# A hybrid decoder block with an expert mixer: which chunks take the dense path, and where the last two chunks are selected

## The chip, the core and the metric

The kernel runs on one core of a Trainium2 chip. Its engines work side by side, each through its own queue in order: TensorE (PE, with PEld for its weight loads), VectorE (DVE), ScalarE (ACT), GpSimd (POOL) and the queue that issues most DMAs (SP). The metric is the device time of one execution in microseconds.

## What is computed

The input is 1024 tokens of width 1024, with 16 meta tokens in front. A mixer (a causal convolution beside a latent attention, both normalised, times `w_out`) is added to the input; the rest is the expert mixer, which works on chunks of 128 tokens:

```python
q = (xb @ wq).reshape(C, PEER_HEADS, 2, PEER_DK_HALF)
s = jnp.einsum('chpd,hpnd->chpn', q, keys).astype(jnp.float32)
sv, si = lax.top_k(s, K)
cand = sv[:, :, 0, :, None] + sv[:, :, 1, None, :]
cidx = si[:, :, 0, :, None] * N_KEYS + si[:, :, 1, None, :]
top_s, sel = lax.top_k(cand.reshape(C, PEER_HEADS, K * K), K)
eidx = jnp.take_along_axis(cidx.reshape(C, PEER_HEADS, K * K), sel, axis=-1)
g = jax.nn.softmax(top_s, axis=-1)
u = u_tab[eidx]
act = jax.nn.gelu(jnp.einsum('chkd,cd->chk', u, xb).astype(jnp.float32), approximate=False)
w = (g * act).astype(xb.dtype)
return jnp.einsum('chk,chkd->cd', w, v_tab[eidx])
```

So each token picks 128 of 16384 experts (8 heads, 16 each), takes a dot product with each expert's row of u, and sums the rows of v with the weights. A last norm with the gain `g_final` follows.

## The kernel before, in words

The eight chunks are worked on in five sets (chunk 0; chunk 1; chunks 2 and 3; 4 and 5; 6 and 7). The string `ORDER` (line 61) says in which order the program is recorded: B is the attention of a set, C its output projection with the scores and the first top 16 (`mix_out`), S its selection (`select`: candidate sums, the second top 16, and the look-up of the expert numbers by comparison `eq` on VectorE, product `ep` on GpSimd and reduction `ef` on VectorE), T its turn (`turn`: the numbers transposed). A scheduler then places each instruction in its engine's queue, by this order and by its own estimate of times; within a queue the order is fixed.

The experts are evaluated in two ways. The chunks in `GATHER` fetch rows: `gather_u` has GpSimd issue, for each of 128 places, an indirect DMA of one row of u per token (`ug`, three buffers), and VectorE multiplies and sums it (`ujunk`, line 691); `gather_v` fetches the rows of v (`vg`, seven buffers) and TensorE sums them (`gv`, line 718). A chunk's v runs beside the next chunk's u; `finish` scales and stores the chunk.

The chunks in `DENSE` take all 16384 experts: E (`expand`) makes a dense table of their gates (VectorE and GpSimd build one-hot factors `one`, `two`, `ah`, `al`, TensorE multiplies them into `pg`, ScalarE copies to `st`, and a DMA writes `g_d`). Then `dense` runs over 128 blocks of 128 experts: `pa` = u times the tokens (24 matmuls of three products of split operands), gelu, times the gates (`ge`, line 818), split into `wh` and `wl` (lines 821 and 822), and after each four blocks `pv` = v times the weights (96 matmuls), added to `acc` on VectorE (line 835). The operands are split (`u_..l`, `v_..l`, line 784) on VectorE. All dense chunks of a block go through one matmul of 512 columns. The gathers run on beside it, 1.1 steps a block as recorded (`RATE`), 32 steps before it (G32).

Before, chunks 0 to 3 are gathered and chunks 4 to 7 dense, so the dense part needs the selection and expansion of the last set.

Of the kernel before, what the change touches and what calls it, by code (L numbers as in the profile page):

```python
# [13 lines left out]
F32 = mybir.dt.float32  # L14
F32R = mybir.dt.float32r
# [20 lines left out]
H = 8  # L36
# [23 lines left out]

ORDER = "B1 C1 S1 B2 C2 T1 S2 B3 C3 T2 S3 B4 X0 C4 T3 E0 E1 Y0 S4 T4 E2 N0 E3 U3 G32 D0"
RATE = 1.1
CONV_POOL = [3]
GATHER = [0, 1, 2, 3]
DENSE = [4, 5, 6, 7]
ND = len(DENSE) * P
# [16 lines left out]
def trunk_kernel(ctx, tc, x, meta, g_mix, w_ab, w_lat, g_q, w_uq, g_kv, w_ukv, conv_w, conv_b,  # L83
# [469 lines left out]
    def mix_out(si, MT):  # L553
# [22 lines left out]

        sv = [sel.tile([P, H, 2, TK], F32, name=f"sv{si}_{j}", tag="sv", bufs=dim.nw) for j in range(nt)]
        sx = [sel.tile([P, H, 2, TK], U32, name=f"sx{si}_{j}", tag="sx", bufs=dim.nw) for j in range(nt)]
        for h in range(H):
# [29 lines left out]

    def select(c, sv, sx):  # L610
        si = sel.tile([P, H, 2, TK], F32, name=f"si{c}", tag="sif", bufs=1)
        V.tensor_copy(si, sx)
# [17 lines left out]
        e = sel.tile([P, H, TK], F32, name=f"ef{c}", tag="ef", bufs=dim.nw)  # L630
        for h in range(0, H, HB):
            for i, n in enumerate((NC1, NCAND)):
                ks = slice(8 * i, 8 * i + 8)
                sh = [P, HB, n, 8]
                eq = sel.tile(sh, F16, name=f"eq{c}_{h}_{i}", tag=f"eq{i}", bufs=2)
                pr = sel.tile(sh, F32, name=f"ep{c}_{h}_{i}", tag=f"ep{i}", bufs=2)
                V.tensor_tensor(eq, tf[:, h:h + HB, None, ks].broadcast_to(sh), iota_c[:, None, :n].broadcast_to(sh), op=OP.is_equal)  # L637
                G.tensor_tensor(pr, eq, cidx[:, h:h + HB, :n, None].broadcast_to(sh), op=OP.mult)
                V.tensor_reduce(e[:, h:h + HB, ks], pr.rearrange("p h c k -> p h k c"), axis=AX.X, op=OP.add)  # L639
        g = sel.tile([P, H, TK], F32, name=f"gg{c}", tag="gg", bufs=dim.nw)  # L640
        gs = sel.tile([P, H], F32, name=f"gs{c}", tag="gs", bufs=1)
# [15 lines left out]
    def turn(c):  # L657

        ef, g = picks[c]
        tp = bank(f"et{c}", (P, 4, P), "s" if c in DENSE else "c")  # L660
        transpose_to(tp[:, 0], ef, P)
        eT = const.tile([P, P], I32, name=f"eT{c}", tag="eT", bufs=5)
        V.tensor_copy(eT, tp[:, 0])
        if c in GATHER:
            chunks[c] += (eT,)
        else:
            transpose_to(tp[:, 1], g.rearrange("p h k -> p (h k)"), P)
            t = sel.tile([P, 4, P], F16, name=f"gd{c}", tag="gd", bufs=len(DENSE))
# [27 lines left out]
    def gather_v(c):  # L696
# [36 lines left out]

    def finish(c, ht):
# [52 lines left out]
    def dense_u(i1, bank):  # L787
# [9 lines left out]
        return ge  # L797

    def dense():
        dn = ctx.enter_context(tc.tile_pool(name="dn", bufs=1, **RW))  # L800
        psd = ctx.enter_context(tc.tile_pool(name="psd", bufs=1, space=PSUM, **RW))

        def pbank(name):
# [6 lines left out]
        for g in range(NK // NG):  # L810
# [3 lines left out]
            for b in range(NG):  # L814
                i1 = NG * g + b
                ge = ges.pop(0) if ges else dense_u(i1, pbank)
                gev = ge.rearrange("p (a t) -> p a t", t=TG)
                V.tensor_tensor(gev, gev, gt[:, :, b], op=OP.mult)
                wh = dn.tile([P, ND], F32R, name=f"wh{i1}", tag="wh", bufs=5)
                wl = dn.tile([P, ND], F32R, name=f"wl{i1}", tag="wl", bufs=4)  # L820
                A.activation(wh, ge, AF.Copy)  # L821
                V.tensor_tensor(wl, ge, wh.bitcast(F32), op=OP.subtract)  # L822
                W.append((wh, wl))
                while done < RATE * (i1 + 1):
                    next(steps, None)
                    done += 1
# [45 lines left out]
    for t in tops[0]:  # L872
        select(*t)
# [5 lines left out]
    dim = SimpleNamespace(nw=NW, nk=NC, wraw=WRAW)  # L879
# [3 lines left out]
    gp = ctx.enter_context(tc.tile_pool(name="gp", bufs=1, side="right", **RW))  # L883
    sel = select_pool()
# [7 lines left out]
    for step in ORDER.split():  # L892
# [90 lines left out]
```

## Time and profile before

| | us |
|---|---|
| median of 3 runs (3037.05 to 3041.81) | 3037.69 |
| the profiled execution | 3034.4 |
| its span in the profile | 3032.6 |
| busy: PE, DVE, ACT, POOL | 2591.0, 2165.6, 1009.9, 1589.2 |
| chain that ended last: PE, DVE, DMA | 49%, 17%, 12% |

The shares of busy time are means over stages with different limits; the slices of the page's second part show TensorE at 5 to 7 tenths in the second quarter and at 9 from the middle on. Matmuls are pipelined, and one has 0.39 us of latency where the next starts earlier, so their pace is read from the distance of starts. A row of `gv` or `ujunk` in the program leaves two records in the trace.

### The profile page before, as it was taken

To read this page: it belongs to the slowest core of one execution; us is meant where nothing else is said; L and a number is where in the kernel's file an instruction comes from. 1 tells how busy PE (TensorE), PEld (TensorE's weight loads), DVE (VectorE), ACT (ScalarE), POOL (GpSimd) and SP (SyncE) were. 2 spreads that over 40 slices of the span, in tenths; PEclk is the share of its full clock that TensorE was granted. 3 is DMA by queue.
4 is the path that set the end of the run, shared out by engine and by line. 5 is a ranking of instruction groups with operands and counts; after the bars stand their busy time and mean duration, and the time that the engine had idled before them with its cause. 6 is when DMAs were issued, how large, how long until landed. Compare 5 with 4: busy or idle time off the path is not lost.

```text
span 3032.6 us, 40483 instructions
## 1 busy us (share of the span) xinstructions
PE 2591.0 (85%) x13295; PEld 1932.6 (64%) x13295; DVE 2165.6 (71%) x4917; ACT 1009.9 (33%) x2200; POOL 1589.2 (52%) x1608
## 2 busy tenths in 40 slices
PE   6878669897876756558998999999999999999996
PEld 6775547776643534336877777777777777776663
DVE  4888857999998999876877766666676656653332
ACT  5435325352520433443222222322232322232221
POOL 5885453534568668662333544544555444534444
PEclk9888858898897877668999999999999999999998
DMA  4114789896788996998888999999999999978886
GB/s 141 46 49 144 227 257 322 261 295 225 246 280 288 314 305 228 315 307 316 300 297 285 326 356 348 332 347 335 346 334 345 337 343 339 352 282 318 311 308 215
DMA packets 372563, 858.36 MB, mean 283 GB/s; under 512 B 37952, under 2 KB 134400, under 8 KB 368256
## 3 DMA queue, kind: packets, MB, share of 16 engines
q0 software_dynamic: 147456, 536.94, 50.9%
q1 hardware_dynamic: 216528, 295.68, 28.7%
q10 hardware_dynamic: 8368, 23.15, 2.1%
q8 instruction: 105, 1.72, 0.2%
q14 instruction: 106, 0.87, 0.1%
HBM read 798.92 MB, written 56.71 MB: 282 GB/s over the span
## 4 chain that ended last, share of the span: by engine, by line
PE 49%; DVE 17%; DMA 12%; issue 4%; POOL 3%; ACT 1%; POOLq 0%; DVEq 0%; ACTq 0%; SPq 0%
PE pv L178 19%; PE pa L178 18%; DMA ug<-in_dram,ei 9%; PE gv L718 7%; DVE ujunk L691 4%; DVE ef L639 2%; DMA vg<-in_dram,eT 1%; PE op L564 1%; DVE two L753 1%; DVE eq L637 1%; DVE ah L755 1%; POOL vg L714 1%; DVE one L754 1%; POOL ug L688 1%; POOL al L756 1%
## 5 line engine op out<-in xcount | busy, mean ns | idle before, releaser
L714 POOL DMA_INDIRECT vg<-in_dram,eT x512 | 559.5, 1093 | 652.6 <-PE gv L718 520.0
L688 POOL DMA_INDIRECT ug<-in_dram,ei x512 | 553.7, 1081 | 584.4 <-DVE ujunk L691 299.6
L691 DVE SCALAR_TENSOR_TENSOR ujunk<-ug,xn 128x1024 bf16<-128x1024 f32 x512 | 638.4, 1247 | 149.4 <-DMA ug<-in_dram,ei 139.1
L835 DVE TENSOR_TENSOR acc<-acc,pv 128x512 f32<-128x512 f32 x256 | 171.9, 685 | 203.5 <-PE pv L178 176.1
L718 PE MATMUL gv<-vg,wd 128*32 128x512 f32 x2048 | 275.6, 653 | 37.5 <-DMA vg<-in_dram,eT 37.4
L178 PE MATMUL pv<-v_0h,wh 128*128 128x512 f32 x512 | 201.3, 398 | 23.9 <-ACT wh L821 16.9
L178 PE MATMUL pv<-v_1l,wh 128*128 128x512 f32 x512 | 200.9, 394 | 3.7 <-DVE v_1l L784 3.7
L178 PE MATMUL pa<-xdh,u_1l 128*128 128x512 f32 x512 | 200.8, 392 | 2.5 <-DVE u_1l L784 2.5
L178 PE MATMUL pa<-xdh,u_0h 128*128 128x512 f32 x512 | 202.1, 395 | 0.3 <-ACT st L764 0.3
L178 PE MATMUL pa<-xdl,u_0h 128*128 128x512 f32 x512 | 201.3, 393 | 0.0
L178 PE MATMUL pa<-xdh,u_0l 128*128 128x512 f32 x512 | 201.2, 393 | 0.0
L178 PE MATMUL pa<-xdh,u_1h 128*128 128x512 f32 x512 | 201.0, 393 | 0.2 <-ACT u_1h L783 0.2
L178 PE MATMUL pa<-xdl,u_1h 128*128 128x512 f32 x512 | 200.4, 391 | 0.0
L178 PE MATMUL pv<-v_0l,wh 128*128 128x512 f32 x512 | 200.3, 395 | 0.0
L178 PE MATMUL pv<-v_1h,wl 128*128 128x512 f32 x512 | 199.9, 392 | 0.0
L178 PE MATMUL pv<-v_1h,wh 128*128 128x512 f32 x512 | 196.5, 396 | 2.8 <-DVE acc L835 2.8
L783 ACT ACTIVATE u_1h<-u_1r 128x512 fp32r<-128x512 f32 x128 | 80.7, 631 | 349.6 <-PE pa L178 251.1
L178 PE MATMUL pv<-v_0h,wl 128*128 128x512 f32 x512 | 194.7, 395 | 0.8 <-DVE wl L822 0.8
L764 ACT ACTIVATE st<-pg 128x256 f32<-128x256 f32 x256 | 130.1, 644 | 190.0 <-PE pg L762 140.7
L783 ACT ACTIVATE u_0h<-u_0r 128x512 fp32r<-128x512 f32 x128 | 80.8, 631 | 322.4 <-PE pa L178 244.9
L761 PE MATMUL pg<-ah,two 128*128 128x128 f16 x512 | 98.0, 271 | 98.2 <-DVE ah L755 82.8
L784 DVE TENSOR_TENSOR u_0l<-u_0r,u_0h 128x512 fp32r<-128x512 f32 x128 | 88.5, 692 | 126.6 <-ACT u_0h L783 89.7
(449 smaller groups left out, 5910.1 us busy)
## 6 DMA issues: line engine op xcount, KB each, us to landing
g_d<-st SPq DMA_DIRECT2D x32, 1024.0 KB
u_0r<-in_dram SPq DMA_DIRECT2D x128, 256.0 KB
u_1r<-in_dram SPq DMA_DIRECT2D x128, 256.0 KB
gt<-g_d SPq DMA_DIRECT2D x32, 1024.0 KB
v_0r<-in_dram SPq DMA_DIRECT2D x128, 256.0 KB
v_1r<-in_dram SPq DMA_DIRECT2D x128, 256.0 KB
wo<-in_dram SPq DMA_DIRECT2D x80, 256.0 KB
wq<-in_dram SPq DMA_DIRECT2D x80, 256.0 KB
```

Source lines behind the costliest of these rows:

```text
L178: PE.matmul(dst, l, r, start=first and j == 0, stop=last and j == 2)
L564: PE.matmul(pb, MT[:, k, j * P:(j + 1) * P], w[k // 2][:, k % 2], start=k == 0, stop=k == KD - 1)
L639: V.tensor_reduce(e[:, h:h + HB, ks], pr.rearrange("p h c k -> p h k c"), axis=AX.X, op=OP.add)
L688: G.indirect_dma_start(out=ug, out_offset=None, in_=u_tab, in_offset=bass.IndirectOffsetOnAxis(ap=ei[:, j:j + 1], axis=0))
L691: V.scalar_tensor_tensor(junk, ug, 1.0, xn, op0=OP.mult, op1=OP.mult, accum_out=dots[:, j:j + 1])
L714: G.indirect_dma_start(out=vg[j], out_offset=None, in_=v_tab, in_offset=bass.IndirectOffsetOnAxis(ap=eT[:, t:t + 1], axis=0))
L718: PE.matmul(acc[32 * j:32 * j + 32, 512 * n:512 * n + 512], w[:, j, 32 * i:32 * i + 32], vg[j][:, 512 * n:512 * n + 512], start=q == 0 and ...
L761: PE.matmul(pg[:, k], two[:, a, :, b], ah[:, a, :, b], start=True, stop=False)
L764: A.activation(st[i][:, :, r0 + r:r0 + r + 4].rearrange("p a b -> p b a"), pg[:, :, i * NK // 2:(i + 1) * NK // 2], AF.Copy, scale=1.0 / G ...
L783: A.activation(hi, raw, AF.Copy)
L784: V.tensor_tensor(lo, raw, hi.bitcast(F32), op=OP.subtract)
L835: V.tensor_tensor(a, a, pv, op=OP.add)
```

## The change

Chunks 2 to 5 become dense, and 0, 1, 6 and 7 are gathered. The expansions E0 to E3 are recorded before the projection of the last set (C4), and S4 and T4 leave the string: the last set's selection, `late_set`, is a generator that the dense part advances twice after each block's `wl`, and `tc.issue_after` ties these steps in order behind that `wl`. Its first-round values live in a pool of their own (`late`), and `select` yields between its pieces. In the dense part the selection's buffers for comparison and product are single, the turn's transposes use the banks of `pa`, and `wh` has four buffers instead of five. The final gain is no longer kept on chip: it is loaded for each gathered chunk, and once for the dense ones, into a buffer of `vg`. The diff, cut:

```diff
-ORDER = "B1 C1 S1 B2 C2 T1 S2 B3 C3 T2 S3 B4 X0 C4 T3 E0 E1 Y0 S4 T4 E2 N0 E3 U3 G32 D0"
+ORDER = "B1 C1 S1 T1 B2 C2 S2 B3 C3 S3 B4 X0 T2 T3 E0 E1 E2 E3 C4 Y0 N0 U3 G32 D0"
...
-GATHER = [0, 1, 2, 3]
-DENSE = [4, 5, 6, 7]
+GATHER = [0, 1, 6, 7]
+DENSE = [2, 3, 4, 5]
+LATE = 4
...
         for h in range(H):
+            if h % 2 == 0:
+                yield
             top16(tv[:, h], ti[:, h], cand[:, h], NCAND)
+        yield
...
         for h in range(0, H, HB):
+            if h and h % 2 == 0:
+                yield
             for i, n in enumerate((NC1, NCAND)):
...
-                eq = sel.tile(sh, F16, name=f"eq{c}_{h}_{i}", tag=f"eq{i}", bufs=2)
-                pr = sel.tile(sh, F32, name=f"ep{c}_{h}_{i}", tag=f"ep{i}", bufs=2)
+                eq = sel.tile(sh, F16, name=f"eq{c}_{h}_{i}", tag=f"eq{i}", bufs=dim.sb)
+                pr = sel.tile(sh, F32, name=f"ep{c}_{h}_{i}", tag=f"ep{i}", bufs=dim.sb)
...
-        tp = bank(f"et{c}", (P, 4, P), "s" if c in DENSE else "c")
+        tp = bank(f"et{c}", (P, 4, P), "c")
...
-        finish(c, ht)
+        finish(c, ht, load_bcast(gp.tile([P, D], F32, name=f"gfin{c}", tag="vg", bufs=7), g_fin))
...
+    def late_set():
+        for t in tops[LATE]:
+            for _ in select(*t):
+                yield
+            turn(t[0])
+
     def dense():
...
+        banks["c"] = (psd, 3, "act")
+        rest = late_set()
...
-                wh = dn.tile([P, ND], F32R, name=f"wh{i1}", tag="wh", bufs=5)
+                wh = dn.tile([P, ND], F32R, name=f"wh{i1}", tag="wh", bufs=4)
...
-                V.tensor_tensor(wl, ge, wh.bitcast(F32), op=OP.subtract)
+                split_done = V.tensor_tensor(wl, ge, wh.bitcast(F32), op=OP.subtract)
                 W.append((wh, wl))
+                with tc.issue_after(split_done.ins):
+                    next(rest, None)
+                    next(rest, None)
                 while done < RATE * (i1 + 1):
...
+        gfin = load_bcast(gp.tile([P, D], F32, name="gfin", tag="vg", bufs=7), g_fin)
         for ci, c in enumerate(DENSE):
-            finish(c, acc[:, ci])
+            finish(c, acc[:, ci], gfin)
...
-    gfin = load_bcast(gp.tile([P, D], F32, name="gfin"), g_fin)
...
             ps_ctx.close()
+            dim.sb = dim.sp = 1
+            sel = ctx.enter_context(tc.tile_pool(name="sel", bufs=1, side="right", **RW))
             dense()
```

Where the instructions stand, at three places. First VectorE's queue at the first dense blocks; `wl0` is the low split of block 0's weights, `v0_1_0l` a split of v, `ge3` block 3's product with the gates, `ujunk` a gathered row, `pv0_0_0` a sum of block group 0. Before:

```order
L784 TENSOR_TENSOR v0_0_0l_12209<-v0_0_0r_12207,v0_0_0h_12208 128x512
L822 TENSOR_TENSOR wl0_11979<-ge0_11366,wh0_11978 128x512
L822 TENSOR_TENSOR wl1_12059<-ge1_11405,wh1_12058 128x512
L784 TENSOR_TENSOR v0_1_0l_12215<-v0_1_0r_12213,v0_1_0h_12214 128x512
L822 TENSOR_TENSOR wl2_12096<-ge2_11444,wh2_12095 128x512
L691 SCALAR_TENSOR_TENSOR ujunk_14342,dots1_12008<-ug1_91_14340,xn1_12006 128x1024
L784 TENSOR_TENSOR v0_2_0l_12221<-v0_2_0r_12219,v0_2_0h_12220 128x512
L818 TENSOR_TENSOR ge3_12168<-ge3_12168,gt0_11975 128x512
L784 TENSOR_TENSOR v0_3_0l_12227<-v0_3_0r_12225,v0_3_0h_12226 128x512
```

After (`si6`, `cand6` are the selection of chunk 6):

```order
L839 TENSOR_TENSOR wl0_11651<-ge0_11035,wh0_11650 128x512
L616 CAST si6_11654<-sx4_0_10571 128x256
L624 TENSOR_TENSOR cand6_11656<-sv4_0_10569 128x8x8
L624 TENSOR_TENSOR cand6_11656<-sv4_0_10569 128x8x4 x3
L624 TENSOR_TENSOR cand6_11656<-sv4_0_10569 128x8x8
L624 TENSOR_TENSOR cand6_11656<-sv4_0_10569 128x8x4
L624 TENSOR_TENSOR cand6_11656<-sv4_0_10569 128x8x3
L624 TENSOR_TENSOR cand6_11656<-sv4_0_10569 128x8x2 x2
L624 TENSOR_TENSOR cand6_11656<-sv4_0_10569 128x8x3
L624 TENSOR_TENSOR cand6_11656<-sv4_0_10569 128x8x8
L839 TENSOR_TENSOR wl1_11770<-ge1_11074,wh1_11769 128x512
L793 TENSOR_TENSOR v0_1_0l_12019<-v0_1_0r_12017,v0_1_0h_12018 128x512
```

Between the splits of blocks 0 and 1 there now stand a cast and the eleven candidate sums of chunk 6's selection; its further pieces, and chunk 7's, follow between the later splits up to block 9.

Second TensorE's queue at block 5; `pa5` is block 5's first product, `pv1` the sum of blocks 4 to 7, `et6` the transpose of chunk 6's expert numbers. Before:

```order
L178 MATMUL pa4_12369<-xdh_9918,u4_1l_12390 128x512
L178 MATMUL pa4_12369<-xdh_9918,u4_1h_12389 128x512
L178 MATMUL pa4_12369<-xdl_9919,u4_1h_12389 128x512
L178 MATMUL pa4_12369<-xdh_9918,u4_1l_12390 128x512
L178 MATMUL pa5_12445<-xdh_9918,u5_0h_12447 128x512
L178 MATMUL pa5_12445<-xdl_9919,u5_0h_12447 128x512
L178 MATMUL pa5_12445<-xdh_9918,u5_0l_12448 128x512
```

After:

```order
L180 MATMUL pv1_0_1_12682<-v1_0_0h_12645,wl4_12214 128x512
L180 MATMUL pv1_0_2_12696<-v1_0_0h_12645,wh4_12213 128x512
L180 MATMUL pv1_0_2_12696<-v1_0_0l_12646,wh4_12213 128x512
L180 MATMUL pv1_0_2_12696<-v1_0_0h_12645,wl4_12214 128x512
L158 MATMUL et6_12247<-ident_111,ef6_11842 128x128
L180 MATMUL pa5_12322<-xdh_10921,u5_0h_12324 128x512
L180 MATMUL pa5_12322<-xdl_10922,u5_0h_12324 128x512
```

The transpose of the selection's result stands ahead of block 5, and chunk 7's in the same way ahead of block 9; before, both stood ahead of block 3, at the start of the last two expansions.

Third the end of VectorE's queue; `os` are the roots for the final scaling, `ht` the last gathered chunk. Before:

```order
L835 TENSOR_TENSOR acc_11970<-acc_11970,pv31_1_2_26337 128x512
L835 TENSOR_TENSOR acc_11970<-acc_11970,pv31_1_3_26351 128x512
L724 TENSOR_TENSOR ht3_25387<-ht3_25387,gv3_22294 128x1024
L736 SCALAR_TENSOR_TENSOR ht3_25387<-ht3_25387,os3_25391,gfin_3872 128x1024
L736 SCALAR_TENSOR_TENSOR acc_11970<-acc_11970,os4_26366,gfin_3872 128x1024
L736 SCALAR_TENSOR_TENSOR acc_11970<-acc_11970,os5_26373,gfin_3872 128x1024
L736 SCALAR_TENSOR_TENSOR acc_11970<-acc_11970,os6_26380,gfin_3872 128x1024
```

After:

```order
L855 TENSOR_TENSOR acc_11642<-acc_11642,pv31_1_1_26335 128x512
L855 TENSOR_TENSOR acc_11642<-acc_11642,pv31_1_2_26349 128x512
L745 SCALAR_TENSOR_TENSOR acc_11642<-acc_11642,os2_26380,gfin_26377 128x1024
L745 SCALAR_TENSOR_TENSOR acc_11642<-acc_11642,os3_26387,gfin_26377 128x1024
L855 TENSOR_TENSOR acc_11642<-acc_11642,pv31_1_3_26363 128x512
L745 SCALAR_TENSOR_TENSOR acc_11642<-acc_11642,os4_26394,gfin_26377 128x1024
L745 SCALAR_TENSOR_TENSOR acc_11642<-acc_11642,os5_26401,gfin_26377 128x1024
```

The last gathered chunk's sum and scaling stood behind the last dense sum and ahead of the dense chunks' scalings; now they stand earlier in the queue, before block 127, and two scalings stand ahead of the last dense sum.

## Rows read from the trace of the kernel before

**Rows 1.** windows by stage: length, busy PE, PEld, DVE, ACT, POOL, clock, DMA

```profile
600.00:882.00 282.00, 243.39 (x1260) 188.81 (x1262) 260.04 (x1021) 125.73 (x371) 135.18 (x156) 0.90 0.83 266
882.00:947.00 65.00, 33.25 (x144) 15.96 (x136) 60.76 (x270) 4.30 (x11) 53.77 (x63) 0.74 0.75 251
947.00:1070.00 123.00, 86.64 (x554) 63.20 (x554) 107.51 (x287) 40.06 (x85) 89.91 (x83) 0.84 0.91 314
1070.00:1210.00 140.00, 81.92 (x535) 54.64 (x536) 136.82 (x436) 48.74 (x98) 101.24 (x104) 0.71 0.78 259
1210.00:1292.00 82.00, 42.97 (x321) 25.45 (x320) 65.77 (x94) 31.56 (x63) 53.81 (x44) 0.66 0.95 318
1292.00:1360.00 68.00, 38.79 (x318) 25.12 (x317) 53.36 (x76) 30.26 (x61) 42.97 (x33) 0.63 0.93 302
1360.00:1397.00 37.00, 21.77 (x104) 16.44 (x104) 15.67 (x24) 7.61 (x15) 15.87 (x14) 0.82 1.00 368
1397.00:1456.00 59.00, 55.88 (x239) 46.14 (x240) 47.39 (x79) 21.68 (x38) 15.72 (x14) 0.94 0.82 287
1456.00:1651.00 195.00, 179.83 (x762) 143.92 (x761) 155.15 (x261) 52.10 (x94) 73.63 (x68) 0.98 0.86 292
1651.00:2994.40 1343.40, 1336.14 (x6509) 970.28 (x6507) 798.47 (x1291) 373.12 (x628) 636.85 (x591) 1.00 0.92 330
2994.40:3032.60 38.20, 9.15 (x49) 1.60 (x48) 8.33 (x7) 5.75 (x10) 13.14 (x17) 0.64 0.54 196
```

**Rows 2.** the windows of line 818 alone: length, busy DVE (x begun), clock, DMA

```profile
1397.00:1456.00 59.00, 5.79 (x9) 0.94 0.82 287
1456.00:1651.00 195.00, 10.25 (x15) 0.98 0.86 292
```

**Rows 3.** who waited for whom, VectorE, 1397 to 1651 us: total, times, longest

```profile
DVE ujunk L691 <- DMA ug<-in_dram,ei: 39.8, 27, 5.7
```

**Rows 4.** VectorE in order of time, the end: start, duration, operation, idle before

```profile
2994.66 0.69 DVE L835 TENSOR_TENSOR acc<-acc,pv 128x512 f32<-128x512 f32 x1 [2.07 <-PE pv L178]
3015.49 1.22 DVE L724 TENSOR_TENSOR ht<-ht,gv 128x1024 f32<-128x1024 f32 x1 [20.15 <-PE gv L718]
3018.90 1.28 DVE L736 SCALAR_TENSOR_TENSOR ht<-ht,os,gfin 128x1024 f32<-128x1024 f32 x1 [2.18 <-POOL os L141]
...
3026.07 1.28 DVE L736 SCALAR_TENSOR_TENSOR acc<-acc,os,gfin 128x1024 f32<-128x1024 f32 x1 [0.44 <-POOL os L141]
```

**Rows 5.** the window of chunk 0's selection: columns as in rows 1

```profile
364.30:390.50 26.20, 1.76 (x9) 1.76 (x9) 24.87 (x107) 0.31 (x1) 14.28 (x28) 0.50 0.63 194
```

**Rows 6.** window of the rows of u (tile ujunk) alone, as rows 2

```profile
1456.00:1651.00 195.00, 82.33 (x134) 0.98 0.86 292
```

**Rows 7.** groups by line, VectorE: busy us, mean ns, idle before by releaser

```profile
L822 DVE TENSOR_TENSOR wl<-ge,wh 128x512 fp32r<-128x512 f32 x128 | 87.9, 689 | 48.5 <-ACT wh L821 33.1 <-PE pv L178 8.7 <-issue 6.4
L818 DVE TENSOR_TENSOR ge<-ge,gt 128x512 f32<-128x512 f32 x128 | 87.3, 685 | 21.5 <-ACT ge L796 12.0 <-DMA gt<-g_d 9.2 <-issue 0.3
```

**Rows 8.** who waited for whom, VectorE, 1210 to 1360 us

```profile
DVE one L754 <- POOL al L756: 26.0, 5, 7.0
```

**Rows 9.** who waited for whom, VectorE, 880 to 1210 us

```profile
DVE ef L639 <- POOL ep L638: 6.4, 4, 5.1
```

**Rows 10.** window of the gather matmuls (tile gv) alone: PE, PEld, DVE first

```profile
1651.00:2994.40 1343.40, 181.87 (x1504) 39.34 (x1504) 3.65 (x3) 1.00 0.92 330
```

**Rows 11.** groups by line, GpSimd: columns as in rows 7

```profile
L688 POOL DMA_INDIRECT ug<-in_dram,ei x512 | 553.7, 1081 | 584.4 <-DVE ujunk L691 299.6 <-issue 59.8 <-DVE mx L505 29.6
L638 POOL TENSOR_TENSOR ep<-eq,cidx 128x160 f32<-128x160 f16 (+1 forms) x128 | 103.7, 823 | 33.5 <-DVE eq L637 32.3 <-DVE tv L604 0.3 <-DVE gs L645 0.2
```

**Rows 12.** TensorE in order of time, first dense matmuls: start, duration

```profile
1369.23 0.63 PE L178 MATMUL pa<-xdh,u_0l 128*128 128x512 f32 x1
1369.66 0.46 PE L178 MATMUL pa<-xdh,u_0h 128*128 128x512 f32 x1
1369.96 0.40 PE L178 MATMUL pa<-xdl,u_0h 128*128 128x512 f32 x1
```

More of the change, by code (lines that the diff above doesn't have):

```diff
@@ L575, in mix_out @@
             to_T(hs[j], P, NT, j * P)
-        sv = [sel.tile([P, H, 2, TK], F32, name=f"sv{si}_{j}", tag="sv", bufs=dim.nw) for j in range(nt)]
-        sx = [sel.tile([P, H, 2, TK], U32, name=f"sx{si}_{j}", tag="sx", bufs=dim.nw) for j in range(nt)]
+        pool = late if si == LATE else sel
+        sv = [pool.tile([P, H, 2, TK], F32, name=f"sv{si}_{j}", tag="sv", bufs=dim.nw) for j in range(nt)]
+        sx = [pool.tile([P, H, 2, TK], U32, name=f"sx{si}_{j}", tag="sx", bufs=dim.nw) for j in range(nt)]
         for h in range(H):
@@ L626, in select @@
         for h in range(H):
+            if h % 2 == 0:
+                yield
             top16(tv[:, h], ti[:, h], cand[:, h], NCAND)
+        yield
         tf = sel.tile([P, H, TK], F16, name=f"tf{c}", tag="tf", bufs=1)
         V.tensor_copy(tf, ti)
[L630 removed]
+        e = sel.tile([P, H, TK], F32, name=f"ef{c}", tag="ef", bufs=dim.sp)
         for h in range(0, H, HB):
+            if h and h % 2 == 0:
+                yield
             for i, n in enumerate((NC1, NCAND)):
@@ L639, in select @@
                 V.tensor_reduce(e[:, h:h + HB, ks], pr.rearrange("p h c k -> p h k c"), axis=AX.X, op=OP.add)
-        g = sel.tile([P, H, TK], F32, name=f"gg{c}", tag="gg", bufs=dim.nw)
+        g = sel.tile([P, H, TK], F32, name=f"gg{c}", tag="gg", bufs=dim.sp)
         gs = sel.tile([P, H], F32, name=f"gs{c}", tag="gs", bufs=1)
@@ L667, in turn @@
             transpose_to(tp[:, 1], g.rearrange("p h k -> p (h k)"), P)
-            t = sel.tile([P, 4, P], F16, name=f"gd{c}", tag="gd", bufs=len(DENSE))
+            t = ex.tile([P, 4, P], F16, name=f"gd{c}", tag="gd", bufs=len(DENSE))
             A.activation(t[:, 0], tp[:, 1], AF.Copy, scale=GSCALE)
             V.scalar_tensor_tensor(t[:, 1], tp[:, 1], GSCALE, t[:, 0], op0=OP.mult, op1=OP.subtract)
-            ii = sel.tile([P, 2, P], I32, name=f"ii{c}", tag="ii", bufs=1)
+            ii = ex.tile([P, 2, P], I32, name=f"ii{c}", tag="ii", bufs=1)
             V.tensor_scalar(ii[:, 0], eT, 7, None, op0=OP.logical_shift_right)
@@ L732, in gather_all, with finish @@
             streams = [gather_v(c) for c in GATHER[k:k + 1]] + [gather_u(c) for c in GATHER[k + 1:k + 2]]
-    def finish(c, ht):
+    def finish(c, ht, gfin):
         r = inv_rms(ht, f"o{c}")
@@ L837, in dense @@
             pass
+        gfin = load_bcast(gp.tile([P, D], F32, name="gfin", tag="vg", bufs=7), g_fin)
         for ci, c in enumerate(DENSE):
-            finish(c, acc[:, ci])
-    dim = SimpleNamespace(nw=1, nk=1, wraw=WRAW0)
+            finish(c, acc[:, ci], gfin)
+    dim = SimpleNamespace(nw=1, nk=1, wraw=WRAW0, sb=2, sp=1)
     al_ctx, cp_ctx, bp_ctx, ex_ctx, sel_ctx, ps_ctx = [ctx.enter_context(ExitStack()) for _ in range(6)]
@@ L872, in trunk_kernel @@
     for t in tops[0]:
-        select(*t)
+        list(select(*t))
         turn(t[0])
@@ L878, in trunk_kernel @@
         c_.close()
-    dim = SimpleNamespace(nw=NW, nk=NC, wraw=WRAW)
+    dim = SimpleNamespace(nw=NW, nk=NC, wraw=WRAW, sb=2, sp=4)
     psv = ctx.enter_context(tc.tile_pool(name="psv", bufs=1, space=PSUM, **RW))
@@ L883, in trunk_kernel @@
     gp = ctx.enter_context(tc.tile_pool(name="gp", bufs=1, side="right", **RW))
+    late = ctx.enter_context(tc.tile_pool(name="late", bufs=1, side="right", **RW))
     sel = select_pool()
@@ L899, in trunk_kernel @@
             for t in tops[i]:
-                select(*t)
+                list(select(*t))
         elif step[0] == "T":
```

## The prediction

> **What bounds the kernel now.** I read the time by stages first, then who waits for whom, then the end. In [rows 1] VectorE is the full engine from 600 to 1397 us (260 of 282 us up to 882, then 440 of 515 us), while TensorE is half idle from 1070 on, with a granted clock of 0.63 to 0.71. From 1651 us it is the other way round: TensorE is busy for 1336.1 of 1343.4 us and VectorE for 798. Between the two lies a mixed stretch. [Rows 2] count the multiplications `ge` by the gates, one for each of the 128 dense blocks: nine begin between 1397 and 1456 us, fifteen between 1456 and 1651. So I call 1397, 1456 and 1651 us the marks ge0, ge9 and ge24. In this stretch VectorE is the one waited for; it is itself idle for 39.8 us between ge0 and ge24 because a gathered row of u has not landed [rows 3], and the split tiles that TensorE needs stand behind that wait. The last stage is a tail: in [rows 4] the last dense sum is added at 2994.66 us, the last gathered chunk's sum only at 3015.49, and the four dense chunks' final scalings stand behind that chunk's, so that the last begins at 3026.07; the span ends at 3032.6.
>
> So there are two sums: VectorE's work up to a mark from which TensorE alone counts, and TensorE's work after it.
>
> **Before ge0.** The change takes the selection of chunks 6 and 7 out. Chunk 0's selection is nearly alone on VectorE in [rows 5]: 24.9 us busy, and some 1.5 us of candidate sums before the row starts (estimate), 26.4 us a chunk, 52.8 for two. In the changed order 73 rows of u instead of 78 stand between the start of S on chunk 4 (882 us before) and ge0, and two u splits fewer. A row of u keeps VectorE for 82.33/67 = 1.23 us [rows 6] (each leaves two records), a split 0.69 [rows 7]: 6.2 and 1.4 us less. Busy time falls from 440 to 380 us. I leave the idle 75 us as they are: the expansions keep their own pace (26 us of waits for GpSimd's half of them in [rows 8]), and the start of the dense part waits for g_d to be written and read again as before. That gives 455 us. Eight rows of u more stand ahead of chunk 4's selection; VectorE is 92% busy there, so 9 of their 9.8 us count, and the selection begins at 891. ge0 comes at 1346 us, 51 earlier. Bounds: with all 75 us of idle filled it is 1271; with each expansion at the 82 us of the slower uncovered one in [rows 1], instead of mostly below it, some 20 us later than 1346.
>
> **ge0 to ge9.** Here both selections now stand between the splits, and the transposes of their results stand in TensorE's queue ahead of blocks 5 and 9, so everything behind them waits for VectorE. Before: 59 us, 47.4 of them busy, with 15 rows of u. After: 52.8 for the selections, 25 rows of u more (30.8), 16 more splits and sums (11.0), the first gathered chunk's closing sum and scaling (2.5): 144.5 us busy. Nearly no wait for rows of u is left, since other work stands between them; for the waits on GpSimd's products (6.4 us over four selections, 880 to 1210 us, [rows 9]) and the switch of chunks I add 10. That is 154.5 us, 95.5 more. Bounds for the waits are 0 and the 61 us of the first rival.
>
> **ge9 to ge24.** 58 rows of u instead of 68 (12.3 us less) and 14 splits and sums fewer (9.7): 133.2 us busy instead of 155.2. Waiting was 39.8 us for 68 rows, 0.59 each, now 34: 167 us, 28 less. TensorE's floor does not bind: 657 dense matmuls at (1336.1-181.9)/5005 = 0.231 us ([rows 1, 10], gathers taken out) are 152 us. Mark ge24 comes at 1346+154.5+167 = 1667.5 us, 16.5 late: VectorE has by then done 21 rows of u more than before, which is work done ahead that nobody needs yet.
>
> **From ge24 on** TensorE has the same work: 5070 dense matmuls in both orders, and 1502 records of gather matmuls against 1504 before the last pv [rows 10]. I keep 1343.4 us, so the last pv ends at 3011. But now all gathers end before block 125, where before most of the 49 matmul records of the last stage in [rows 1] were gathers behind the last pv. Behind it are left one sum, the square, the root and the scaling (0.3+0.7+2.2+1.3), one scaling that queues (1.3) and the store, 5.25 us from the last scaling's end to the span's end [rows 4]: 11, I take 12, against 38.2 before [rows 1]. The tail gives back 26 us.
>
> **Edits at nothing.** One buffer fewer for `wh`: `wl` already has four, and waits for TensorE 8.7 us in all 128 blocks [rows 7]; between 0 and another 8.7. The five loads of the final gain instead of one: the first scaling stands in ge0 to ge9, so a late landing would hold VectorE, as gt's does for 9.2 us once [rows 7]; the others lie under TensorE's full stretch. SP's loads queued behind them wait no longer than for the gather buffer that the closing load waits for already. Single product buffers are in the 10 us.
>
> Sum: 3032.6 + 16.5 - 26.2 = 3022.9 us of span. The profiled execution took 3034.4, 1.8 over its span, and the median of the runs is 3037.69, 3.3 over that: **3028 us**.
>
> **Rivals.**
> *The selection stalls behind GpSimd (slower).* With one buffer each, a comparison, GpSimd's product and the reduction of a head are a chain, and the products share GpSimd's queue with the gathers' issues. Each of 32 pairs would wait for one issue and one product, 1.08+0.82 us [rows 11]: 61 us, span and time +58 beyond the few us in my sum, 3086; for half the pairs 3057. From 0.3 us a pair on it eats the gain. For it: the longest such wait was 5.1 us [rows 9]. Against: then four waits in 64 pairs, and other VectorE work stands between most pairs. 0.2.
>
> *TensorE starts cold.* In the expansions it was busy for about half the time, and [rows 1] grant 0.63 and 0.66 of the clock; the first dense matmuls still start 0.43 us apart [rows 12], against 0.231 later: the levels 1.2 and 2.4 GHz. Between the two transposes stand 192 dense matmuls: 83 us at 0.43 against some 70 us of VectorE work. If the half level holds there, +13: 3041. Against it: once the matmuls came unbroken the pace rose, 0.43 and then 0.30 us in neighbouring rows of [rows 12], and the next stage but one was granted 0.94. 0.08. The Trainium skill (TensorE: Matmul & The Clock Gate, "HAM oscillation — how this bites in real kernels") says that matmul groups cut by waits can each start at the half level again, which speaks against this change. By that rule the time would be the 3041 just worked out; these rows agree that half-idle stretches were granted the lower level.
>
> *VectorE's waits fill up better (faster).* If ge9 to ge24 runs at TensorE's floor (152 instead of 167) and a tenth to a quarter of the idle 75 us before ge0 goes, 3028-15-8 to -19, about 3000. For it: the selection's small pieces gave VectorE its fullest stage, 136.8 of 140 us. Against: the expansions keep less beside them now. 0.22.
>
> That the change does not do what it says I leave out: its order shows both selections between the first dense blocks' splits.
>
> **Chances.** Forecast 0.5, with 3012 to 3041 for its own range (idle before ge0 by 20 either way, the waits beside the selections by 10). A measurement tells 0.2%, 6 us, from no change. Faster than 3031.6: 0.31 of the forecast's 0.5 and the fuller VectorE's 0.22, 0.53. Within: 0.14 and most of the cold case, 0.19. Slower than 3043.8: the stall's 0.2, 0.03 of the cold case, 0.05 of mine: 0.28. The range reaches to the fuller case and past the stall of half the pairs, 2998 to 3062.
>
> **What would show it.** ge0 near 1346; the 24.9 us of a selection twice between ge0 and ge9, that stretch near 155 us with VectorE over 90% busy; ge24 some 15 us later than before; TensorE full from there for about 1343 us; the last pv followed by the end within 12 us. A wait of the reduction for GpSimd's product of over 15 us, a dense part that starts after 1370, or TensorE idle past ge24 would make it wrong.

## The result: slower, with the loss ahead of everything the sum had worked out

The changed kernel took 3075.07 us (median of 4 runs, 3069.37 to 3080.8), the kernel before 3039.75 beside it: ratio 1.011, 95% interval 1.0094 to 1.0126. The prediction was 3028 us, with a range up to 3062: wrong in its sign and outside its range. The profiled execution of the changed kernel took 3075.31 us, with a span of 3073.5, 40.9 longer than before.

The windows between the marks of the prediction (start of chunk 4's selection, ge0, ge9, ge24, end of the last pv), for the changed kernel, answer to [rows 1]: length, then busy time of PE, PEld, DVE, ACT, POOL (instructions), granted clock, DMA share, GB/s.

```profile
600.00:926.90 326.90, 281.39 (x1413) 215.50 (x1414) 274.23 (x1047) 126.61 (x369) 154.82 (x180) 0.88 0.84 277
926.90:1387.40 460.50, 279.27 (x1935) 189.74 (x1933) 380.85 (x943) 161.36 (x335) 303.30 (x266) 0.75 0.91 307
1387.40:1544.20 156.80, 99.86 (x387) 69.92 (x388) 138.89 (x382) 34.44 (x56) 100.65 (x107) 0.79 0.75 256
1544.20:1713.20 169.00, 159.92 (x684) 127.99 (x684) 135.79 (x227) 50.36 (x87) 65.28 (x60) 0.99 0.87 300
1713.20:3062.30 1349.10, 1339.26 (x6513) 972.33 (x6511) 772.45 (x1247) 374.03 (x632) 603.00 (x566) 1.00 0.90 321
3062.30:3073.50 11.20, 0.24 (x2) 0.00 (x0) 4.36 (x4) 1.29 (x4) 2.93 (x5) 0.75 0.46 187
```

Read the lengths first. The five stages behind 926.9 last 460.5, 156.8, 169.0, 1349.1 and 11.2 us; predicted were 455, 154.5, 167, 1343.4 and 12. The one mark that is far off is the first: 926.9 instead of 891. The shares say what kind of stage it is: up to there VectorE was busy 92% of the time before [rows 1], and now 274 of 327 us, 84%. It does only 14 us more there, in a stretch that is 45 us longer; the rest is waiting.

The other rows of before have their answers in the changed kernel as follows. Nine and fifteen multiplications by the gates still begin between the marks [rows 2], and with them go 193 records of rows of u, 96 rows for the 98 of the sum [rows 6]. Waits for a row of u between ge0 and ge24 are 41.4 us where they were 39.8 [rows 3], and waits of the reduction for GpSimd's product are 3.4 in that stretch, with two selections in it [rows 9] (VectorE's waits, 1387 to 1713 us: total, times, longest):

```profile
DVE ujunk L700 <- DMA ug<-in_dram,ei: 41.4, 29, 5.4
...
DVE ef L648 <- POOL ep L647: 3.4, 2, 3.0
```

The gather matmuls of the long last stage take what they took in [rows 10], and VectorE's splits, with one buffer fewer for `wh`, what they took in [rows 7] (window of gv alone; VectorE's group of the splits):

```profile
1713.20:3062.30 1349.10, 181.87 (x1502) 39.33 (x1502) 3.65 (x3) 1.00 0.90 321
```

```profile
L839 DVE TENSOR_TENSOR wl<-ge,wh 128x512 fp32r<-128x512 f32 x128 | 88.1, 688 | 57.0 <-ACT wh L838 43.1 <-PE pv L180 8.8 <-issue 4.9
```

The missing buffer shows in the queue of ScalarE, which writes `wh`. Its waits for TensorE there are longer than before; first the group before, then in the changed kernel:

```profile
L821 ACT ACTIVATE wh<-ge 128x512 fp32r<-128x512 f32 x128 | 80.4, 629 | 184.9 <-DVE ge L818 151.9 <-PE pv L178 26.8 <-DVE u_0l L784 3.5
```

```profile
L838 ACT ACTIVATE wh<-ge 128x512 fp32r<-128x512 f32 x128 | 80.4, 629 | 277.2 <-DVE ge L835 123.2 <-PE pv L180 101.9 <-PE gv L727 29.3
```

A cost in time is not seen. Of the runs below, t1_early keeps the five buffers and its long last stage takes 1349.0 us; t1_late, t1_bank and mix12 have four buffers and as many records of gather matmuls in that stage (1536), and take 1346 to 1352.

And the tail is as forecast (VectorE in order of time; compare [rows 4]): no closing sum of a gathered chunk is left, and two scalings follow the last dense sum, the second after a wait for its root.

```profile
3060.91 1.28 DVE L745 SCALAR_TENSOR_TENSOR acc<-acc,os,gfin 128x1024 f32<-128x1024 f32 x1 [0.36 <-POOL os L143]
...
3064.10 0.68 DVE L855 TENSOR_TENSOR acc<-acc,pv 128x512 f32<-128x512 f32 x1
3064.70 1.28 DVE L745 SCALAR_TENSOR_TENSOR acc<-acc,os,gfin 128x1024 f32<-128x1024 f32 x1
3066.97 1.28 DVE L745 SCALAR_TENSOR_TENSOR acc<-acc,os,gfin 128x1024 f32<-128x1024 f32 x1 [1.00 <-POOL os L143]
```

**Where the front loses its time.** Both kernels run alike up to some 440 us; C1's first matmul then starts at 446.0 us before and at 454.9 after. The large step comes next: C2, the projection of chunks 2 and 3, starts at 538.8 us before and at 602.9 after (its first weight load; the first matmul follows 0.2 to 0.3 us later). TensorE in order of time, first the kernel before, with T1's transpose `et`, then the changed kernel around C2's start:

```profile
539.06 2.48 PE L564 MATMUL op<-wo,mt 128*128 128x256 f32 x5
...
704.27 0.48 PE L156 MATMUL et<-ident,ef 128*128 128x128 f32 x1 [4.88 <-ACT s L595]
```

```profile
602.88 0.47 PE L158 MATMUL et<-ident,ef 128*128 128x128 f32 x1 [5.92 <-DVE ef L648]
603.15 3.19 PE L566 MATMUL op<-wo,mt 128*128 128x256 f32 x7
```

The `et` is T1, the transpose of chunk 1's list, which waits for the last reduction of chunk 1's selection; the projection's first matmul stands right behind it. T1 is recorded ahead of C2 in the changed order string, and both take their result tile from the same two PSUM buffers (tag c). Before, T1 ran at 704.3 us, long after C2. What that does to the engines is seen in the windows 550 to 605 and 605 to 710 us, first of the kernel before, then of the changed one:

```profile
550.00:605.00 55.00, 48.59 (x242) 38.59 (x241) 53.04 (x168) 20.48 (x63) 35.88 (x46) 0.93 0.82 258
605.00:710.00 105.00, 87.13 (x429) 67.52 (x427) 94.29 (x369) 46.08 (x152) 38.27 (x43) 0.89 0.92 289
```

```profile
550.00:605.00 55.00, 37.04 (x133) 28.68 (x134) 53.17 (x186) 18.29 (x61) 33.40 (x44) 0.52 0.55 167
605.00:710.00 105.00, 93.86 (x464) 76.61 (x463) 72.28 (x228) 42.20 (x137) 34.48 (x37) 0.89 0.90 286
```

First TensorE has less to do: 109 matmuls fewer, at a mean granted clock of 0.52 of full speed, close to the lower of its two levels. Then it is VectorE: 72.3 us instead of 94.3. What is missing there is the search for the top scores `sv`, whose scores come from the projection. Its instructions in the second window alone, before and after, are 22.8 us apart:

```profile
605.00:710.00 105.00, 39.81 (x240) 0.89 0.92 289
```

```profile
605.00:710.00 105.00, 17.05 (x104) 0.89 0.90 286
```

These 22 us are not made up by the first mark, in a stage where VectorE is the full engine.

### The profile page after: what moved, and what is told of

It is laid out like the page before. It is cut to its first block, busy times and chain, and to the rows that moved or that the text cites. A ratio compares the mean times of both kernels' runs of the same rounds, so it can differ in the third digit from the quotient of the medians.

```text
span 3073.5 us, 40510 instructions
## 1 busy us (share of the span) xinstructions
PE 2594.7 (84%) x13295; PEld 1931.4 (63%) x13295; DVE 2162.2 (70%) x4917; ACT 1013.7 (33%) x2204; POOL 1586.8 (52%) x1608
## 5 line engine op out<-in xcount | busy, mean ns | idle before, releaser
L727 PEld LDWEIGHTS gv<-vg,wd 128*32 128x32 f32 x2048 | 56.1, 114 | 189.1 <-issue 130.4
L838 ACT ACTIVATE wh<-ge 128x512 fp32r<-128x512 f32 x128 | 80.4, 629 | 277.2 <-DVE ge L835 123.2
```

The lines of the kernel that those rows point to most:

```text
L727: PE.matmul(acc[32 * j:32 * j + 32, 512 * n:512 * n + 512], w[:, j, 32 * i:32 * i + 32], vg[j][:, 512 * n:512 * n + 512], start=q == 0 and ...
```

## The experiments

Two theories stood at the start. **A:** T1's tile of tag c holds up C2, and that is the front's loss. **B, C:** it is something else in the front (rows of u, pools). As the results came in a third was needed, **E:** from the first dense block on there are two chains, the dense blocks and the gathers, and the span ends with the later. The marks of all profiled executions, in us, and the ratios of the runs:

| kernel | C2 | chunk 4's selection | ge0 | ge24 | last pv ends | last gv ends | span | ratio to before (95%) |
|---|---|---|---|---|---|---|---|---|
| before | 538.8 | 882.7 | 1396.7 | 1650.9 | 2994.4 | 3015.2 | 3032.6 | 1 |
| changed | 602.9 | 926.9 | 1387.4 | 1713.2 | 3062.3 | 3020.8 | 3073.5 | 1.0110 (1.0094 to 1.0126) |
| t1_late | 547.5 | 893.8 | 1348.7 | 1678.8 | 3030.4 | 3022.5 | 3040.8 | 1.0032 (1.0019 to 1.0046) |
| t1_bank | 550.1 | 904.5 | 1359.1 | 1694.9 | 3043.2 | 3011.9 | 3054.4 | 1.0059 (1.0039 to 1.0079) |
| t1_early | 597.4 | 916.7 | 1411.5 | 1668.2 | 3017.2 | 3007.4 | 3026.9 | 0.9948 (0.9934 to 0.9961) |
| thin | 547.4 | 894.6 | 1345.0 | 1603.5 | 2940.8 | 3014.2 | 3031.7 | 1.0011 (0.9996 to 1.0026) |
| one | 546.9 | 891.2 | 1346.4 | 1656.7 | 2996.9 | 3011.7 | 3029.2 | 0.9975 (0.9961 to 0.9988) |
| sel_out2 | 552.0 | 900.5 | 1404.8 | 1652.3 | 2996.3 | 3031.0 | 3048.5 | 1.0035 (1.0024 to 1.0047) |
| one_early | 602.0 | 923.9 | 1376.9 | 1678.4 | 3023.0 | 3006.9 | 3034.3 | 1.0011 (0.9993 to 1.0028) |
| mix12 | 552.9 | 900.4 | 1355.1 | 1682.3 | 3028.6 | 3024.0 | 3041.5 | 1.0016 (1.0000 to 1.0032) |
| one_c4 | 549.7 | 900.4 | 1356.5 | 1678.1 | 3025.0 | 3020.5 | 3037.9 | 0.9985 (0.9970 to 0.9999) |
| one_fin | 549.8 | 895.7 | 1350.0 | 1662.0 | 3002.4 | 3020.5 | 3030.8 | 0.9977 (0.9966 to 0.9989) |

C2 is the start of its first weight load. A mark of one execution is good to some 5 us: up to chunk 4's selection seven of these kernels (T1 late, no other edit there) have the same order, and they reach it between 891.2 and 900.5. The spans of single profiled executions scatter likewise, so verdicts go by the ratios.

### T1 back behind C2 (t1_late)

```diff
-ORDER = "B1 C1 S1 T1 B2 C2 S2 B3 ...
+ORDER = "B1 C1 S1 B2 C2 T1 S2 B3 ...
```

> The changed kernel, with T1 (the transpose of chunk 1's finished list) back behind C2 in the order string, and nothing else. Theory A (T1 takes one of the two PSUM buffers of tag c before C2 asks for them, so C2's projection waits for the whole selection of chunk 1): C2's projection starts near 540 us instead of 602.9, chunk 4's selection 30 to 40 us earlier than the 926.9 of the changed kernel, total about 3037 us (3028 to 3045). Rival B (more rows of u and their waits in the front are what delays chunk 4's selection): projection of set 2 may move, chunk 4's selection stays near 920 us, total 3065 to 3078. Rival C (other pools and buffers): as B, about 3075.

Measured: 3048.74 us (10 runs). C2's first matmul on TensorE, then the stages in the profile:

```profile
547.72 1.46 PE L566 MATMUL op<-wo,mt 128*128 128x256 f32 x6
```

```profile
600.00:893.80 293.80, 252.90 (x1290) 194.92 (x1288) 263.38 (x1027) 131.05 (x385) 145.90 (x168) 0.88 0.82 267
893.80:1348.70 454.90, 281.61 (x1928) 186.51 (x1926) 379.10 (x937) 159.38 (x332) 305.53 (x266) 0.76 0.92 312
1348.70:1507.70 159.00, 95.89 (x371) 70.71 (x372) 142.62 (x380) 34.59 (x56) 96.28 (x103) 0.78 0.74 248
1507.70:1678.80 171.10, 159.75 (x683) 127.78 (x681) 136.62 (x230) 48.79 (x85) 67.86 (x60) 0.99 0.87 295
1678.80:3030.40 1351.60, 1342.36 (x6547) 972.86 (x6545) 788.00 (x1273) 374.64 (x633) 623.88 (x585) 1.00 0.91 327
3030.40:3040.80 10.40, 0.28 (x2) 0.00 (x0) 4.04 (x4) 2.10 (x4) 1.68 (x4) 0.69 0.50 200
```

C2 starts 55 us earlier, chunk 4's selection 33 us, and the later stages last as long as they did, within 6 us: moving one step in the order string gives back 26 us of time. A stands, B and C fall for the larger part. The total is 4 us over A's range: with T1 late the kernel is still 0.3% slower than before, so T1 is not the whole loss.

### T1 early, its tile from other buffers (t1_bank)

```diff
-        tp = bank(f"et{c}", (P, 4, P), "c")
+        tp = psv.tile([P, 4, P], F32, name=f"et{c}", tag="gv", bufs=1) if c == 1 else bank(f"et{c}", (P, 4, P), "c")
```

> The changed kernel with T1 where the change puts it, but with its transpose written to a buffer of the gathers' PSUM pool (unused until the first gathered sum), not to one of the two of tag c. Theory A: it is the buffer, not the place in the order, so the projection of set 2 starts near 540 us again, total as with T1 behind C2, 3030 to 3045. If it is the place in TensorE's queue itself: the projection stays near 600, total near 3075.

Measured: 3056.76 us, 12 us over the range of A. TensorE in order of time:

```profile
550.39 2.83 PE L566 MATMUL op<-wo,mt 128*128 128x256 f32 x12
...
607.36 0.47 PE L158 MATMUL et<-ident,ef 128*128 128x128 f32 x1 [4.91 <-DVE ef L648]
```

T1 still waits until 607 us, but the projection no longer stands behind it: it starts at 550.4. So it was the tile of tag c, not the place in the order string, that tied C2 to the selection. 18 of the 26 us come back. For the other 8 the traces show a place: up to chunk 4's selection VectorE works on 150 rows of u here, and on 142 with T1 late (rows of u alone, two records each, t1_bank first).

```profile
0.00:904.50 904.50, 186.09 (x300) 0.86 0.65 207
```

```profile
0.00:893.80 893.80, 176.61 (x284) 0.86 0.65 206
```

These eight rows are 9.5 us of VectorE, and the mark comes 10.7 us later. That they are the cause is not shown, since no run moves them alone and the marks scatter by as much. By which rule the two buffers are handed out is not shown, only that C2 comes free when T1's tile leaves them. The Trainium skill (Perfetto Trace Analysis, "Optimization Strategy") says that gaps which repeat on the engine that should be full can mean too few buffers for the next tile. Here the gap came once, on an engine that was not the full one (TensorE, 37.0 of 55 us busy), and it was the other engine that paid.

### T1 early in the kernel before (t1_early)

```diff
-ORDER = "B1 C1 S1 B2 C2 T1 S2 B3 ...
+ORDER = "B1 C1 S1 T1 B2 C2 S2 B3 ...
```

> The kernel before, with T1 moved ahead of B2 and C2 in the order string, and nothing else: all selections and the dense chunks as before. Theory A: C2's projection starts near 600 us instead of 538.8, chunk 4's selection near 920 instead of 882.7, total 3070 to 3090 us, slower than before by 30 to 50. Rivals B and C: no change, 3035 to 3045.

Measured: 3024.52 us (8 runs), 0.5% *faster* than before, where A expected 30 to 50 us more. The first half is as A says: C2 at 597.4, chunk 4's selection 34 us late. Before, the stage up to ge0, then the stages here:

```profile
882.70:1396.70 514.00, 304.64 (x1966) 200.68 (x1962) 439.14 (x1178) 162.54 (x331) 357.18 (x336) 0.73 0.87 294
```

```profile
916.70:1411.50 494.80, 290.38 (x1916) 195.30 (x1916) 445.45 (x1181) 161.46 (x328) 344.56 (x328) 0.76 0.88 301
...
1668.20:3017.20 1349.00, 1340.82 (x6545) 971.89 (x6543) 794.36 (x1278) 378.73 (x634) 624.42 (x589) 1.00 0.91 328
3017.20:3026.90 9.70, 0.24 (x2) 0.00 (x0) 3.29 (x4) 1.15 (x2) 1.48 (x4) 0.67 0.43 172
```

The stage up to ge0 takes 494.8 us instead of 514: VectorE's idle time in it is 49 us instead of 75, so more than half of the delay falls into idle time (why there, and not in the changed kernel, where 80 us of idle stayed, I have not tested). What is left makes the last pv 23 us later, but in the kernel before the last pv was not the end: the gathers were, 21 us behind it, and four scalings behind those. They end 8 us earlier here, which is not explained, and the tail behind the last pv falls from 38.2 to 9.7 us. A delay of the dense chain cost nothing, since that chain was not the later one. A was right on the mechanism and wrong on its price, which depends on which chain ends last.

### The selection spread thinner (thin, one, mix12)

```diff
-                    next(rest, None)
-                    next(rest, None)
+                    if b % 2:
+                        next(rest, None)
```

(thin, with T1 late; one has a plain `next(rest, None)` at each block, mix12 one and two in turn.)

> The changed kernel with T1 behind C2, and one piece of the selections of chunks 6 and 7 at every second dense block, instead of two pieces at every block. Theory A plus 'the last stretches were rightly summed as VectorE's work up to ge24': the selection costs VectorE its 53 us before ge24 wherever it stands there, total as with T1 behind C2 alone, 3030 to 3040. Theory D (behind ge0 the bound is TensorE as soon as its queue isn't stopped by the transposes of the selections): ge0 near 1351, then 1598 us to the last pv as in the kernel before, and a tail of 11: 2963 us; a part of that, 2975 to 3015, if some of the stops stay.

Measured: 3042.41 us, the time before: 2 us over the first theory's range, and 79 over D's 2963. The stages from ge0:

```profile
1345.00:1402.90 57.90, 57.22 (x253) 45.20 (x254) 48.30 (x123) 20.02 (x37) 26.59 (x28) 0.97 0.91 331
1402.90:1603.50 200.60, 185.37 (x801) 145.12 (x800) 173.92 (x374) 60.04 (x103) 91.20 (x95) 0.98 0.83 285
1603.50:2940.80 1337.30, 1322.28 (x6393) 968.64 (x6392) 833.88 (x1380) 370.62 (x627) 645.95 (x594) 1.00 0.92 328
2940.80:3031.70 90.90, 32.39 (x146) 5.35 (x144) 8.33 (x7) 5.75 (x10) 37.45 (x43) 0.60 0.68 237
```

D's marks come, but not its end: ge0 at 1345, ge0 to ge24 in 258.5 us instead of 330, the last pv 90 us earlier than with T1 late alone. But 144 records of gather matmuls are left behind it, and the tail grows from 10 to 91 us. Where the 72 us come from shows in what VectorE did between ge0 and ge24, rows of u alone, t1_late first, then thin:

```profile
1348.70:1678.80 330.10, 125.30 (x200) 0.89 0.81 272
```

```profile
1345.00:1603.50 258.50, 85.10 (x138) 0.98 0.85 295
```

Two records a row, so 31 rows fewer, and a part of the selection's pieces later. That work is not saved: it moves behind ge24, where VectorE is busy for 834 of 1337 us. The gathers end at 3014.2 us, no later than with two pieces a block (3022.5), but now they are the end. This led to theory E, and E to numbers for the pace between:

> T1 behind C2, and one piece of the selections of chunks 6 and 7 at every dense block (so that chunk 6's transpose stands behind block 8, chunk 7's behind block 16) instead of two. Theory E (from the first dense block on there are two chains, the dense blocks and the gathers, which share TensorE; the span ends with the later one: dense last with two pieces a block, 3030.4 us, gathers last with half a piece, 3014.2 and the finish behind them): the two end close together, last pv at 2985 to 3005, last gather matmul at 3000 to 3012, total 3015 to 3030 us. Rival F (VectorE's work up to ge24 sets the time wherever the selection stands): last pv near 3030, total 3040 to 3050.

Measured: 3031.47 us (ratio 0.9975), last pv at 2996.9, last gather matmul at 3011.7, both in E's ranges; the time is 1.5 us over its range. Theory F (VectorE's work up to ge24 sets the time, 3040 to 3050) falls. With T1 late and half the pace of the selection the change is thus faster than the kernel before.

> T1 behind C2, and one and two pieces of selection at dense blocks in turn, between the kernel with one a block (last pv 2996.9, last gather matmul 3011.7) and the kernel with two (3030.4 and 3022.5). Theory E: last pv 3008 to 3018, no gather behind it, total 3022 to 3035 us. Rival F (the pieces' place does not matter once they stand before ge24): as with two a block, 3045 to 3050.

Measured: 3043.97 us, with the last pv at 3028.6: a miss for E (3022 to 3035, last pv at 3008 to 3018), and 1 us below F's range (3045 to 3050). At one and a half pieces a block ge24 is as late as with two (1682.3 against 1678.8). E's rule for the end nearly holds (12.9 us behind the last pv instead of 10, no gather behind it); interpolating the chain's length between two settings does not.

### Both edits crossed (one_early), and the selection outside (sel_out2)

one_early is one with T1 ahead of B2; sel_out2 is t1_late with `E0 E1 C4 E2 S4 T4 E3` in the order string and no selection in the dense part.

> One piece of selection a block, and T1 at the early place of the change (ahead of B2 and C2). Theory E with A: chunk 4's selection 30 to 38 us later than the 891.2 of the kernel with T1 late, last pv 3025 to 3038 instead of 2996.9, past the gathers, whose finish of 17.5 us then falls away for 10: total 3038 to 3052 us, 10 to 20 more, less than the 26 that the place of T1 costs where the dense chain is last anyway. If T1's place costs its whole delay here too: 3062 to 3070; if nothing: 3031.

Measured: 3044.13 us, last pv at 3023.0, span 11.3 us behind it: the total as E has it, the last pv 2 us ahead of its range. So T1's early place costs 26 us where the dense chain is last anyway, 13 where the gathers were last by 15 us, and gains 15 in the kernel before.

> T1 behind C2, and the selections of chunks 6 and 7 (with the projection that feeds them) put back among the expansions, ahead of the dense part; the four dense chunks stay 2 to 5. Theory A with E: what then is left of the change is which chunks are dense; first multiplication by the gates at 1395 to 1420 us, nine blocks in 60 instead of 159, last pv near 2995, gathers last near 3010, total 3030 to 3042 us, the time before. Rival: taking the middle chunks costs by itself (later expansions, less to hide behind them): total 3050 to 3065.

Measured: 3052.11 us. ge0 (1404.8), the nine blocks in 61.4 us and the last pv (2996.3) are as expected; the gathers are not, at 3031.0 instead of some 3010, and they are the end. The total lies in the rival's range (3050 to 3065): taking chunks 2 to 5 alone, with the selections outside, is 0.35% slower than before. Why the gathers are late is open. The lists of chunks 6 and 7 do not hold them up: these are turned at 1289 and 1342 us, while the second gathered chunk's last row of u comes only at 1546, and that was 1517 before.

### The end by itself (one_c4, one_fin)

```diff
+        gfin = load_bcast(gu.tile([P, D], F32, name="gfin", tag="ug", bufs=3), g_fin)
+        for ci, c in enumerate(DENSE):
+            finish(c, acc[:, ci], gfin)
         for _ in steps:
             pass
-        gfin = load_bcast(gp.tile([P, D], F32, name="gfin", tag="vg", bufs=7), g_fin)
-        for ci, c in enumerate(DENSE):
-            finish(c, acc[:, ci], gfin)
```

(one_fin: the dense chunks' finish ahead of the last gather step, which is held back to here; one_c4 is one with C4 named behind E1.)

> As the kernel with one piece of selection a block, but with the last set's projection (C4) named behind the second of the four expansions instead of behind the fourth; in its order no gather matmul is left behind the last pv (32 records were before). Theory E (the span ends with the later chain, 10 us behind the last pv or 17.5 us behind the last gather matmul): last gather 3005 to 3012, last pv 3000 to 3012, total 3018 to 3030 us. Rival G (the gathers run at their own pace whatever stands beside them, some 3010 to 3015, and their finish behind): 3030 again.

> The kernel with one piece of selection a block, with the four dense chunks' final scalings ahead of the last gathered chunk's closing sum and scaling in each queue instead of behind them (their gain goes to a buffer of the gathered rows of u, free by then). Theory E: the last gather matmul stays at 3005 to 3015, what follows it falls from 17.5 us (closing sum, its scaling, four scalings that queue, the store) to 10 to 11 (closing sum, one scaling, the store), total 3021 to 3028 us, 7 less than the 3031.5 of the kernel without it. If the end is set by something else behind the gathers (stores, the transfers themselves): 3030 to 3033.

one_c4 took 3034.98 us: no gather is left behind the last pv, but that comes at 3025.0, 13 later than expected, so the total is over both figures. Against one the dense chain is 9 us late at chunk 4's selection, 10 at ge0, 21 at ge24 and 28 at the last pv; why is open. one_fin took 3032.53 us, no gain over one, and in the range of its rival (3030 to 3033). Its mechanism came, in VectorE's order of time:

```profile
3011.61 1.28 DVE L745 SCALAR_TENSOR_TENSOR acc<-acc,os,gfin 128x1024 f32<-128x1024 f32 x1 [4.85 <-POOL os L143]
3020.82 1.22 DVE L733 TENSOR_TENSOR ht<-ht,gv 128x1024 f32<-128x1024 f32 x1 [7.92 <-PE gv L727]
3024.23 1.28 DVE L745 SCALAR_TENSOR_TENSOR ht<-ht,os,gfin 128x1024 f32<-128x1024 f32 x1 [2.19 <-POOL os L143]
```

10.3 us follow the last gather matmul instead of 17.5, but in this execution the gathers ended 9 us later than in one, of which 4 to 5 were there at ge0 and ge24 already. Whether the rest is scatter or a cost of the edit stays open.

## Why the prediction was wrong, step by step

**The step that failed** is the first mark: "Eight rows of u more stand ahead of chunk 4's selection; VectorE is 92% busy there, so 9 of their 9.8 us count, and the selection begins at 891." It took the move of T1 in the order string as free, and priced the front by VectorE's rows of u alone. The runs put in its place a wait: T1's tile ties C2 to the end of chunk 1's selection (t1_late, t1_bank), VectorE runs out of scores, and the mark comes at 926.9. With the tile elsewhere it comes at 904.5, with T1 late at 893.8. Of the 50.6 us by which the span is over the predicted 3022.9, T1's place is 32.7 (3073.5 less t1_late's 3040.8); by the medians, 26.3 of 47. The eight rows themselves are there, 152 ahead of the mark in the changed kernel and 144 before. That the kernels with T1 late show the 891 after all (891 to 900) is luck: 142 rows stand ahead there, two fewer than before, and their delay is another one. C1's first matmul starts at 454 to 457 us in every kernel made from the changed one, 446.0 before, and 18 rows of u stand ahead of it on VectorE instead of 15.

**The other 18 us of the span** are sizes, read from t1_late against the sum. The first mark 2.8; to ge0 nothing (454.9 for 455, with the idle 75.8 us that the sum left as they were); ge0 to ge9 4.5 (159.0 for 154.5); ge9 to ge24 4.1 (171.1 for 167); from ge24 to the last pv 8.2 (1351.6 for 1343.4); the tail -1.6. The term of 1343.4 was the one most off: in the seven kernels with no gather behind the last pv that stage took 1345 to 1352, in the five with 32 to 144 gather records left behind it 1337 to 1344. The forecast set the gathers' records at 1502 for 1504 and kept the length. The changed kernel has these 1502, and the 5.7 us more are not explained (TensorE busy 3.1 longer, idle 2.6). t1_late has 1536 there, and 2.8 us more of gather matmuls.

**The two selections in the dense part** cost what they were said to (95.5 us more in ge0 to ge9 by the sum; 97.8 in the changed kernel), but not by the same terms: VectorE is busy 138.9 us of 156.8, not 144.5, which is 89% and not over 90, and idle 17.9 instead of 10. What was missed is that this price is one of placing. TensorE's queue stands behind the first turn for 19.7 us, as its waits from 1387 to 1544 us show; the second turn comes without a gap here.

```profile
PE et L158 <- DVE ef L648: 19.7, 1, 19.7
PE pv L180 <- DVE acc L855: 18.7, 6, 5.4
PE pv L180 <- ACT wh L838: 9.7, 3, 8.6
```

With a quarter of the pieces at each block those nine blocks took 57.9 us. I called the 21 rows of u done ahead "work done ahead that nobody needs yet". For the dense chain that was right, but the gathers need it: thin, with 31 rows fewer by ge24 than t1_late, has 144 gather records left behind its last pv.

**The rivals.** The selection did not stall behind GpSimd: 3.4 us of waits, not 61. VectorE's waits did not fill up: 79.7 us idle before ge0, where the sum left 75, and 33.2 between ge9 and ge24, where it left 34. TensorE did run at a lower mean clock where its queue was cut: 0.79 between ge0 and ge9, so in part at the lower of its two levels, against 0.97 there in thin. The Trainium skill (TensorE: Matmul & The Clock Gate, "HAM oscillation — how this bites in real kernels") says that matmul groups cut by waits can each start at the half level again, and these rows agree with it. The 13 us worked out for this are not seen: the stage took 2.3 us more than the sum, and VectorE was the busier engine in it. None of the three rivals was what happened. T1's move stood in the diff, and no case had it. One of the prediction's own signs did show: the dense part started after 1370, at 1387.4.

**The tail** was right in length, 11.2 us for 12, with the gathers ahead of the last pv. But the forecast wanted them some 40 us ahead of a last pv at 3011, and no kernel shows that: in all twelve the last gather matmul ends between 3006.9 and 3031.0 us, wherever the last pv ends (2940.8 to 3062.3). In the changed kernel the gathers came first because the dense chain was late. What sets their pace was not tested; the DMA engines are 0.90 to 0.92 busy in the long stage of every kernel whose rows are shown. The 26 us it gives back were real and were spent: the dense chain, 21 us ahead of the gathers before, ended 41 behind them.

## What to carry to other kernels

When a step moves in the order in which a program is recorded, look at every pool that it takes a buffer from, and ask who takes the next one: a small step that waits for one engine can hold up a large step of another that has nothing to do with it. Where two chains share the engines to the end, say which ends last and by how much before pricing a delay: the same early T1 cost 26 us, cost 13, or came with a gain of 15. Work tied into a full stage can be priced by its busy time only if it is also said how thinly it is spread; here half the pace took the change from slower than before to a little faster, while the fastest kernel was the one before with T1 early (0.9948).
